# Three stages of an SSD scan, of three successive slices, issued as one row of small products

## The chip, the cores and the metric

The kernel runs on one core of a Trainium2 chip. The metric is the time of one execution on the device in microseconds (us), the median of several runs. A core has TensorE (PE) with its weight loads (PEld), VectorE (DVE), ScalarE (ACT), GpSimd (POOL) and the queues that start DMAs (SP). Each works through its own instructions in order and waits for others by semaphores.

## The reference, cut to what matters

One step of a two-layer streaming encoder. The change concerns the mixer of layer 0, a Mamba-2 SSD scan (state-space duality) over 1088 positions: 1024 of a new stream and 64 of a running one, whose state h0 is given.

```python
# ssd_mixer: u @ w_in gives z, x/B/C and dt; x/B/C go through a conv of width 4 and silu
y, h_final = ssd_scan(xs, dt, A, Bm, Cm, h0)
y = y + xs * D_skip
y = y * silu(z)
yg = y * rsqrt(mean(y * y over a group of 512 channels) + eps) * gnorm_w
return yg @ w_out

# ssd_scan, by chunks of positions; Acs is the cumulative sum of dt * A in a chunk
Lm = exp(where(causal, Acs[q] - Acs[s], -inf))
y_diag = (C B^T * Lm) @ (x * dt)                        # inside a chunk
chunk_states = B^T @ (x * dt * exp(Acs[-1] - Acs))      # what a chunk adds to the state
h[c + 1] = h[c] * exp(Acs[-1]) + chunk_states[c]        # over the chunks
y_off = (C @ h[c]) * exp(Acs)                           # from the state before
y = y_diag + y_off
```

Then follow a feed-forward layer, shared keys and values, and a layer of attention with its feed-forward layer, which the change doesn't touch.

## The kernel before, in words

**Tiles.** Positions lie along the free axis, in three slices `SL` of 384, 384 and 320, channels along the 128 partitions. The scan takes chunks of 128 positions (`CHL`, nine, the last of 64), so a slice holds three. The 2048 channels of x are 16 tiles j of two heads each. A slice of a tile is numbered q = 3 j + s, 48 in all; below, "slice q" means this.

**Large products.** `unit` (L401) makes one tile of x, z, B or C for one slice: 24 products in `passes` (L386, the rows of L394, L395 and L396), since each factor is split in a high and a low part and three of the four combinations are taken over 8 blocks of k. `passes` and `unit` go through the tiles in the loop at L1011 to L1030: x of tile j, z of tile j − 1, for each slice, and B and C for each four tiles. The result is scaled by the norm of the input (`scaled`, L677, DVE). x, B and C go through `Conv` (L687: craw, then four steps in cvt, L715 and L717, DVE, then Silu on ACT), z through Silu on ACT (tile zs). The weights are cast and split as they come in (L296 ACT, L297 DVE, tile hl).

**Small products.** `group_task` (L730) prepares B and CB of a group, `ssd_task` (L758) the scan of one slice. It is a generator of four stages:

- A: PE transposes x (xtp, L769) and spreads the cumulative sums over the partitions (bcp, L786); DVE makes xd (x dt, L779) and dm (L791), POOL xe (L780), ACT the Exp into ea (L795) and dm (L796), DVE dm times CB (L797).
- B: PE makes the states of the three chunks (sp, L805); DVE carries the state on (hn, L816, L819); for the last chunk SP loads the state of the running stream (h, L811), and hn is stored (L826, L828).
- C: PE makes the two parts of the output (yp, L836, from dm and xd; yo, L845, from the states and C); DVE makes y (L847) and ea times yo (L849), POOL adds them (L850).
- D: POOL multiplies by silu(z) (L856), SP stores y (L857), squares are summed by group in ssg (ACT L863 and L866, POOL L867). In the last tile of a group `rstd` turns these sums into the norm (nst on PE, L427, then the nv chain on DVE from L433).

**What sets the order.** PE runs in the order in which the code issues its instructions. `Stream` (L80) keeps a clock of estimated work; `passes` and `unit` advance it and let every waiting generator go on whose delay has passed and whose condition holds. This happens after each 12 large products, so stages stand between half units as rows of small products. The stages' delays, `SSD_GAP` and the counters in `so` decide between which. The instructions of the other engines are put in order by a scheduler, in which a block under `tc.high_priority(HIP)` goes first. Tiles have few buffers: xd, xe and ea two each, dm four (two per slice), y and h six, zs three, cvt one; in PSUM two each for xtp, sp and others (`ax`), for bcp, and for yp and yo.

**Behind it.** While the last slices run, `build_y` (L634) takes y up again: dg (L448) and nbp (L456) spread the norm, L541 to L543 scale and split y into r, and `project` (L656) multiplies by the output weights, in quarters of the positions, first for half of the channels. At the start, `start_norm` makes the norm of the input with the same nst, nv, dg and nbp.

Of the kernel before, what the change touches and what calls it, by code (L numbers as in the profile page):

```python
# [8 lines left out]
F32 = mybir.dt.float32  # L9
# [3 lines left out]
ALU = mybir.AluOpType  # L13
# [3 lines left out]
P = 128  # L17
D = 1024
# [11 lines left out]
CHL = [128] * 8 + [64]  # L30
HEADS = 32
XT = 16
# [8 lines left out]
RB_WAIT = 4.8  # L41
CHW = ((13.1, 8.8, 18.0), (7.5, 6.0, 17.2)), ((9.0, 5.2, 14.6), (10.5, 6.0, 19.7))
AT_W1, AT_W2 = 6.0, 2.5
SSD_GAP, SSD_D = 4.4, 6.5
ST_W, ST_RB = (6.5, 22.0, 22.0), 1.0
TB_W, TB_V = 1.0, 18.0
ES = 0.5, 0.5, 0.0
# [3 lines left out]
HIP = 3000  # L51
# [20 lines left out]
C_D = 208  # L72
# [246 lines left out]
def hybrid_kernel(  # L319
# [4 lines left out]
    nc = tc.nc  # L324
    V, A, G, PE = nc.vector, nc.scalar, nc.gpsimd, nc.tensor
    ctx.enter_context(tc.manual_schedule(engines={mybir.EngineType.PE}))
    st = Stream()
# [45 lines left out]
    def col(c):  # L373
        return pcs[:, c:c + 1]

    def ax(name):
        return pax.tile([P, 512], F32, tag="ax", name=name)
# [204 lines left out]
    with ExitStack() as es:  # L582
        pbc = es.enter_context(tc.tile_pool(reuse_waits="tile", name="pbc", bufs=2, space=PSUM))
        pyy = es.enter_context(tc.tile_pool(reuse_waits="tile", name="pyy", bufs=2, space=PSUM))
        sb1 = es.enter_context(tc.tile_pool(reuse_waits="tile", name="sb1", bufs=1))
        sb2 = es.enter_context(tc.tile_pool(reuse_waits="tile", name="sb2", bufs=2))
# [35 lines left out]
        dt, acs, dec, cd = tab("dt"), tab("acs"), tab("dec"), tab("cd")  # L622
        tabs = []
# [6 lines left out]
        def table_task():  # L630
# [31 lines left out]
            for s, (o, n) in enumerate(SL):  # L662
                ps = ax("acT")
                for i in range(3):
                    c = 3 * s + i
                    L = CHL[c]
                    PE.transpose(ps[:32, i * P:i * P + L], acs[:L, c, :], ident[:L, :L])
# [5 lines left out]
        rbs = [sb1.tile([P, 384], F32, name=f"rb{s}") for s in range(NSL)]  # L673

        def scaled(dst, ps, s, a, n):

            V.tensor_tensor(dst, ps[:, a:a + n], rbs[s][:, a:a + n], op=ALU.mult)  # L677

        def dt_unit(us, n, pl, tg):
            ps = pl.tile([P, 512], F32, tag=tg, name="dtp")  # L680
# [71 lines left out]
        bc_t = {}  # L752
        cb_done = []
        hst = {}
        so = dict(A=0, B=0, C=0, D=0, tA=0, tC=0)
        ssgs = {}

        def ssd_task(j, s):  # L758
            g, jj = divmod(j, 4)
            xsT = pair_t[j].dst[s]  # L760
            CT = grp_t[g][1].dst[s]
            o, n = SL[s]
            q = 3 * j + s
            yield 0, 0, lambda: tabs and (g, s) in cb_done and so["A"] == q and so["C"] >= q - 1 and st.t >= so["tA"]
            Bn, CB = bc_t[g, s]

            pt = ax("xtp")
            for i in range(3):
                PE.transpose(pt[:, i * P:(i + 1) * P], xsT[:, i * P:(i + 1) * P], ident)  # L769
            xd = sb2.tile([P, 3, P], F32, tag="xd", name="xd")  # L770
            xe = sb2.tile([P, 3, P], F32, tag="xe", name="xe")

            def hd(ap):
                return ap.rearrange("p a (h d) -> p a h d", d=64)

            def tb(t_):
                return t_[:, 3 * s:3 * s + 3, 2 * j:2 * j + 2].unsqueeze(3).to_broadcast([P, 3, 2, 64])

            V.tensor_tensor(hd(xd), hd(pt[:, :384].rearrange("p (a b) -> p a b", b=P)), tb(dt), op=ALU.mult)  # L779
            G.tensor_tensor(hd(xe), hd(xd), tb(dec), op=ALU.mult)  # L780
            MT = []
            ea = sb2.tile([P, 384], F32, tag="ea", name="ea")
            for e in range(2):
                hh = 2 * j + e
                bp = pbc.tile([P, 512], F32, tag="bc", name="bcp")
                PE.matmul(bp[:, :n], sel[:, hh:hh + 1].to_broadcast([P, P]), acr[:, o:o + n], start=True, stop=True)  # L786
                dm = sb2.tile([P, 384], F32, tag="dm", bufs=4, name="dm")
                for i in range(3):
                    c = 3 * s + i
                    L = CHL[c]  # L790
                    V.scalar_tensor_tensor(  # L791
                        dm[:, i * P:i * P + L], bp[:, i * P:i * P + L], acs[:, c, hh:hh + 1], mask[:, :L],
                        op0=ALU.subtract, op1=ALU.min,
                    )
                A.activation(ea[64 * e:64 * e + 64, :n], bp[64 * e:64 * e + 64, :n], AF.Exp)  # L795
                A.activation(dm[:, :n], dm[:, :n], AF.Exp)  # L796
                V.tensor_tensor(dm[:, :n], dm[:, :n], CB[:, :n], op=ALU.mult)  # L797
                MT.append(dm)
            so["A"] = q + 1
            so["tA"] = st.t + SSD_GAP  # L800
            yield 0.7, 4.5, lambda: so["B"] == q

            sp = ax("sp")
            for i in range(3):
                PE.matmul(sp[:, i * P:(i + 1) * P], Bn[:, i, :], xe[:, i, :], start=True, stop=True)  # L805
            hs = []
            for i in range(3):
                c = 3 * s + i
                if c == 8:
                    hst[j] = sb2.tile([P, P], F32, tag="h", bufs=6, name="h")  # L810
                    nc.sync.dma_start(hst[j], h0T[:, j * P:(j + 1) * P])  # L811
                h = hst.get(j)
                hs.append(h)
                hn = sb2.tile([P, P], F32, tag="h", bufs=6, name="hn")
                if c == 0:
                    V.tensor_copy(hn, sp[:, :P])  # L816
                else:
                    for e in range(2):
                        V.scalar_tensor_tensor(  # L819
                            hn[:, 64 * e:64 * e + 64], h[:, 64 * e:64 * e + 64],  # L820
                            cd[:, c, 2 * j + e:2 * j + e + 1], sp[:, i * P + 64 * e:i * P + 64 * e + 64],
                            op0=ALU.mult, op1=ALU.add,
                        )
                hst[j] = hn
                if c == 7:
                    nc.sync.dma_start(hp_o[:, j * P:(j + 1) * P], hn)  # L826
                if c == 8:
                    nc.sync.dma_start(hs_o[:, j * P:(j + 1) * P], hn)  # L828
            so["B"] = q + 1
            yield 0.8, 3.5, lambda: so["C"] == q and so["D"] >= q - 5 and st.t >= so["tC"]  # L830

            yp = pyy.tile([P, 512], F32, tag="yy", name="yp")
            for i in range(3):
                L = CHL[3 * s + i]
                for e in range(2):
                    PE.matmul(  # L836
                        yp[64 * e:64 * e + 64, i * P:i * P + L], xd[:, i, 64 * e:64 * e + 64],
                        MT[e][:, i * P:i * P + L], start=True, stop=True,
                    )
            yo = pyy.tile([P, 512], F32, tag="yy", name="yo")  # L840
            for i in range(3):
                c = 3 * s + i
                L = CHL[c]
                if c > 0:
                    PE.matmul(yo[:, i * P:i * P + L], hs[i], CT[:, i * P:i * P + L], start=True, stop=True)  # L845
            y = sb2.tile([P, 384], F32, tag="y", bufs=6, name="y")
            V.scalar_tensor_tensor(y[:, :n], xsT[:, :n], col(C_D + j), yp[:, :n], op0=ALU.mult, op1=ALU.add)  # L847
            q0 = P if s == 0 else 0
            V.tensor_tensor(ea[:, q0:n], yo[:, q0:n], ea[:, q0:n], op=ALU.mult)  # L849
            G.tensor_tensor(y[:, q0:n], y[:, q0:n], ea[:, q0:n], op=ALU.add)  # L850
            so["C"] = q + 1
            so["tC"] = st.t + SSD_GAP
            yield 1.5, 0, lambda: (j, s) in zst and so["D"] == q
            so["D"] = q + 1

            G.tensor_tensor(y[:, :n], y[:, :n], zst[j, s][:, :n], op=ALU.mult)  # L856
            nc.sync.dma_start(yd_[:, j, o:o + n], y[:, :n])  # L857
            if jj == 0 and s == 0:
                ssgs[g] = sb2.tile([P, NCH * P], F32, tag="ssg", bufs=1, name="ssg")
                G.memset(ssgs[g][:, T:], 0.0)  # L860
            ssg = ssgs[g]
            if jj == 0:
                A.activation(ssg[:, o:o + n], y[:, :n], AF.Square)  # L863
            else:
                sq = nsb.tile([P, 384], F32, tag="sq", bufs=2, name="sq")
                A.activation(sq[:, :n], y[:, :n], AF.Square)  # L866
                G.tensor_tensor(ssg[:, o:o + n], ssg[:, o:o + n], sq[:, :n], op=ALU.add)  # L867
            if jj == 3:
                yield 0, 5.0
                rstd(ssg[:, s * 384:(s + 1) * 384], 1.0 / 512, rst[:, 3 * s:3 * s + 3, g], 3)  # L870
                rst_done.add((g, s))
                yield 0.3, 0

        zst = {}
# [35 lines left out]
        for s, (o, n) in enumerate(SL):  # L910
            xs = []
            if s == 0:
                nc.sync.dma_start(pcs, pc)
                for m in range(0, KD, 3):
                    w_ = min(3, KD - m)
# [67 lines left out]
        for s in range(NSL):  # L983
            us, n = u[s], SL[s][1]
# [5 lines left out]
            for i in range(3):  # L990
                ps = mm("mm") if i else pl.tile([P, 512], F32, tag=tg, name="mmp")
# [19 lines left out]
        for grp in order:  # L1011
# [6 lines left out]
            for i, s in seq:  # L1018
                kd_, jj_ = grp[i]
                q = 3 * jj_ + s  # L1020
# [404 lines left out]
    with ExitStack() as es:  # L1425
        psS = es.enter_context(tc.tile_pool(reuse_waits="tile", name="psS", bufs=2, space=PSUM))
        sb2 = es.enter_context(tc.tile_pool(reuse_waits="tile", name="sba2", bufs=2))
# [237 lines left out]
        for j in range(1, 8):  # L1665
# [4 lines left out]
            for s in range(NSL):  # L1670
                n = SL[s][1]
# [138 lines left out]
```

## Time and profile before

| what | us |
|---|---|
| median of 3 runs | 3126.31 (3126.17 to 3128.03) |
| the profiled execution | 3128.07 |
| its span | 3126.40 |
| PE busy | 2999.5 (96%) |
| DVE busy | 2183.2 (70%) |
| ACT busy | 1361.3 (44%) |
| POOL busy | 932.8 (30%) |

The profile is of one execution. The span runs from its first instruction to its last; an engine's share is its busy time over the span. A mean over stages with different limits says little on any one of them, so the stretch of the scan, about 85 to 710 us, is read by itself. "Waits" are the times in which an engine stood idle for another, with the line that waited and the line that released it. A granted clock of 1.00 is TensorE at full speed. In the timeline, a row's first number is the start and the second the duration; products overlap, so that the distance of two starts is what a product costs.

### The profile page before, as it was taken

To read this page: it belongs to the slowest core of one execution; us is meant where nothing else is said; L and a number is where in the kernel's file an instruction comes from. 1 tells how busy PE (TensorE), PEld (TensorE's weight loads), DVE (VectorE), ACT (ScalarE), POOL (GpSimd) and SP (SyncE) were. 2 spreads that over 40 slices of the span, in tenths; PEclk is the share of its full clock that TensorE was granted. 3 is DMA by queue.
4 is the path that set the end of the run, shared out by engine and by line. 5 is a ranking of instruction groups with operands and counts; after the bars stand their busy time and mean duration, and the time that the engine had idled before them with its cause. 6 is when DMAs were issued, how large, how long until landed. Compare 5 with 4: busy or idle time off the path is not lost. (4 is left out here: it accounts for less than half of the span.)

```text
span 3126.4 us, 56643 instructions
## 1 busy us (share of the span) xinstructions
PE 2999.5 (96%) x21721; PEld 2913.4 (93%) x21721; DVE 2183.2 (70%) x4712; ACT 1361.3 (44%) x2424; POOL 932.8 (30%) x1026
## 2 busy tenths in 40 slices
PE   7999999999998999999998999999998999999998
PEld 7899999989998999999987888888998999999997
DVE  8888888886788555584566788887778655476545
ACT  5545454554443222344443554444544232244432
POOL 3333333331344433441133001100155333342112
PEclk9999999999999999999999999999999999999999
DMA  3111111124533222245654111112344222245654
GB/s 107 40 56 51 57 50 58 50 83 143 170 123 105 78 77 82 86 145 175 200 184 122 53 62 59 57 54 64 127 144 132 74 73 80 77 127 170 204 184 135
DMA packets 174495, 321.80 MB, mean 103 GB/s; under 512 B 17136, under 2 KB 124528, under 8 KB 174224
## 3 DMA queue, kind: packets, MB, share of 16 engines
q1 hardware_dynamic: 174160, 318.11, 32.7%
q8 instruction: 171, 2.80, 0.4%
q14 instruction: 100, 0.82, 0.1%
q0 software_dynamic: 64, 0.07, 0.0%
HBM read 255.51 MB, written 62.60 MB: 102 GB/s over the span
## 5 line engine op out<-in xcount | busy, mean ns | idle before, releaser
L297 DVE TENSOR_TENSOR hl<-raw,hl 128x1024 fp32r<-128x1024 f32 (+1 forms) x297 | 366.0, 1233 | 323.4 <-ACT hl L296 319.8
L394 PE MATMUL mm<-r,hl 128*128 128x384 f32 (+2 forms) x1664 | 563.2, 338 | 10.1 <-DVE kf L1469 9.1
L396 PE MATMUL mm<-r,hl 128*128 128x384 f32 (+2 forms) x1664 | 541.9, 326 | 1.1 <-DVE hl L297 1.1
L395 PE MATMUL mm<-r,hl 128*128 128x384 f32 (+2 forms) x1664 | 541.3, 325 | 0.0
L296 ACT CAST hl<-raw 128x1024 fp32r<-128x1024 f32 (+1 forms) x300 | 303.5, 1014 | 316.8 <-DMA raw<-in_w_f_dram 125.8
L420 POOL TENSOR_TENSOR ssum<-ssum,sq 128x288 f32<-128x288 f32 (+3 forms) x188 | 221.9, 1183 | 565.4 <-ACT sq L419 559.4
L1209 PE MATMUL px<-r,hl 128*128 128x288 f32 (+1 forms) x1192 | 349.6, 293 | 0.0
L394 PEld LDWEIGHTS mm<-r,hl 128*128 128x128 f32 x1664 | 318.1, 191 | 18.8 <-issue 8.2
L395 PEld LDWEIGHTS mm<-r,hl 128*128 128x128 f32 x1664 | 318.3, 191 | 0.9 <-issue 0.5
L396 PEld LDWEIGHTS mm<-r,hl 128*128 128x128 f32 x1664 | 317.3, 191 | 1.4 <-DVE hl L297 1.4
L1208 PE MATMUL px<-r,hl 128*128 128x288 f32 x1056 | 311.4, 295 | 4.4 <-DVE u L1223 4.4
L1210 PE MATMUL px<-r,hl 128*128 128x288 f32 x1056 | 310.7, 294 | 0.0
L1210 PE MATMUL px<-rx,hl 128*128 128x256 f32 x816 | 230.4, 282 | 17.9 <-DVE hl L297 17.9
L1208 PE MATMUL px<-rx,hl 128*128 128x256 f32 x816 | 230.8, 283 | 0.7 <-ACT hl L296 0.7
L1209 PEld LDWEIGHTS px<-r,hl 128*128 128x128 f32 x1192 | 223.9, 188 | 0.0
L1370 PE MATMUL po<-rx,hl 128*128 128x384 f32 (+1 forms) x640 | 207.1, 324 | 0.9 <-DVE rx L1272 0.9
L1208 PEld LDWEIGHTS px<-r,hl 128*128 128x128 f32 x1056 | 198.4, 188 | 6.0 <-DVE u L1223 5.8
L1371 PE MATMUL po<-rx,hl 128*128 128x384 f32 (+1 forms) x608 | 197.0, 324 | 2.0 <-DVE hl L297 2.0
L1369 PE MATMUL po<-rx,hl 128*128 128x384 f32 (+1 forms) x608 | 198.6, 327 | 0.1
L1210 PEld LDWEIGHTS px<-r,hl 128*128 128x128 f32 x1056 | 198.3, 188 | 0.0
L1209 PE MATMUL px<-rx,hl 128*128 128x256 f32 x680 | 191.8, 282 | 0.0
L256 POOL TENSOR_TENSOR tt<-raw 128x512 f32<-128x512 f32 x44 | 61.5, 1397 | 426.3 <-DMA raw<-in_w_f_dram 287.0
(337 smaller groups left out, 8136.0 us busy)
## 6 DMA issues: line engine op xcount, KB each, us to landing
raw<-in_w_f_dram SPq DMA_DIRECT2D x204, 512.0 KB, 3.7
raw<-in_w_in_dram SPq DMA_DIRECT2D x40, 512.0 KB, 3.7
raw<-in_w_f_dram SPq DMA_DIRECT2D x48, 384.0 KB, 3.2
sg<-hscr SPq DMA_DIRECT2D x88, 192.0 KB, 3.5
raw<-in_w_so_dram SPq DMA_DIRECT2D x32, 512.0 KB, 3.8
raw<-in_w_kv_dram SPq DMA_DIRECT2D x16, 512.0 KB, 3.7
raw<-in_w_o_dram SPq DMA_DIRECT2D x16, 512.0 KB, 3.8
sg<-hscr SPq DMA_DIRECT2D x44, 160.0 KB, 3.6
```

What stands on the lines that cost most here:

```text
L296: self.nc.scalar.copy(h, v)
L297: (eng or self.eng or self.nc.vector).tensor_tensor(lo, v, h, op=ALU.subtract)
L394: PE.matmul(ps[:, :n], h_, xh, start=(first and i == 0), stop=False)
L395: PE.matmul(ps[:, :n], h_, xl, start=False, stop=False)
L396: PE.matmul(ps[:, :n], l_, xh, start=False, stop=(last and i == nk - 1))
L420: (eng or G).tensor_tensor(ssum[:, :n], ssum[:, :n], q[:, :n], op=ALU.add)
L1208: PE.matmul(ps, wh, ah[:, k, :], start=(k == 0), stop=False)
L1209: PE.matmul(ps, wh, al[:, k, :], start=False, stop=False)
L1210: PE.matmul(ps, wl, ah[:, k, :], start=False, stop=(k == 3))
L1369: PE.matmul(ps[:, :n], wh, xh, start=(k == 0), stop=False)
L1370: PE.matmul(ps[:, :n], wh, xl, start=False, stop=False)
L1371: PE.matmul(ps[:, :n], wl, xh, start=False, stop=(k == FT - 1))
```

## The change

B and C of a slice become functions, `states` and `outputs`, kept in `stages[q]`. When A of slice q is issued, C of slice q − 2 and B of slice q − 1 are issued just ahead of it, so that a row holds C, B and A of three successive slices. The distance of two rows grows with `SSD_GAP` from 4.4 to 9.5; `SSD_W` and `SSD_E` are the delays after which a slice's later stages are issued by themselves, should no further A have done it. A may run up to two slices ahead of C (before, one), and D must wait for its C. The evacuation `scaled` gets the high priority.

```diff
-SSD_GAP, SSD_D = 4.4, 6.5
+SSD_GAP, SSD_D = 9.5, 6.5
+
+SSD_W, SSD_E = (15.0, 14.0), (4.5, 3.5)
...
         def scaled(dst, ps, s, a, n):
-            V.tensor_tensor(dst, ps[:, a:a + n], rbs[s][:, a:a + n], op=ALU.mult)
+            with tc.high_priority(HIP):
+                V.tensor_tensor(dst, ps[:, a:a + n], rbs[s][:, a:a + n], op=ALU.mult)
...
+        stages = {}
+
+        def later(q, key):
+            if so[key] != q or q not in stages or (key == "C" and so["B"] <= q):
+                return 0
+            cost = stages[q][key]()
+            so[key] = q + 1
+            return cost
...
-            yield 0, 0, lambda: tabs and (g, s) in cb_done and so["A"] == q and so["C"] >= q - 1 and st.t >= so["tA"]
+            yield 0, 0, lambda: (
+                tabs and (g, s) in cb_done and so["A"] == q and so["C"] >= q - 2 and st.t >= so["tA"]
+                and so["D"] >= q - 7
+            )
+
+            cost = 0.7 + later(q - 2, "C") + later(q - 1, "B")
...
             so["tA"] = st.t + SSD_GAP
-            yield 0.7, 4.5, lambda: so["B"] == q
+            def states():       # B: sp, hn, the DMAs of the states, as before
...
-            yield 0.8, 3.5, lambda: so["C"] == q and so["D"] >= q - 5 and st.t >= so["tC"]
+            def outputs():      # C: yp, yo, y, ea, as before
...
-            yield 1.5, 0, lambda: (j, s) in zst and so["D"] == q
+            out = {}
+            stages[q] = dict(B=states, C=outputs)
+
+            w_ = SSD_E if q == 3 * XT - 1 else SSD_W
+            yield cost, w_[0]
+            yield later(q - 1, "C") + later(q, "B"), w_[1] if so["C"] == q else 0, lambda: so["D"] >= q - 5
+            yield later(q, "C"), 0, lambda: (j, s) in zst and so["D"] == q and so["C"] > q
```

What it makes of the order, at three places. On PE in the steady part, four successive rows of small products before (the large products between them are left out):

```order
L805 MATMUL sp<-xe,Bn 128x128 x3
...
L769 MATMUL xtp<-ident,xsT 128x128 x3
L786 MATMUL bcp<-acr,sel 128x384 x2
...
L836 MATMUL yp<-dm,xd 64x128 x4
L836 MATMUL yp<-dm,xd 64x64 x2
L845 MATMUL yo<-CT,hn 128x128 x2
L845 MATMUL yo<-CT,h 128x64
...
L805 MATMUL sp<-xe,Bn 128x128 x3
```

and a row in the same part now:

```order
L856 MATMUL yp<-dm,xd 64x128 x4
L856 MATMUL yp<-dm,xd 64x64 x2
L865 MATMUL yo<-CT,hn 128x128 x2
L865 MATMUL yo<-CT,h 128x64
L823 MATMUL sp<-xe,Bn 128x128 x3
L787 MATMUL xtp<-ident,xsT 128x128 x3
L804 MATMUL bcp<-acr,sel 128x384 x2
```

B, A and C stood 12 large products apart here; in other places before, two or three of them stood together. Now every row has all three, 48 large products behind the row before it. Before, five rows held three slices' stages, now three do.

On PE in the tail, between units of the first projection, the rows around the norm of the last tile before (nst; six, for two slices):

```order
L394 MATMUL mm<-r,hl 128x256
L395 MATMUL mm<-r,hl 128x256
L396 MATMUL mm<-r,hl 128x256
L427 MATMUL nst<-ones,ssg 128x1 x6
L456 MATMUL nbp<-dg,frac 128x256
L394 MATMUL mm<-r,hl 128x256
```

and now:

```order
L398 MATMUL mm<-r,hl 128x256
L856 MATMUL yp<-dm,xd 64x128 x4
L856 MATMUL yp<-dm,xd 64x64 x2
L865 MATMUL yo<-CT,hn 128x128 x2
L865 MATMUL yo<-CT,h 128x64
L458 MATMUL nbp<-dg,frac 128x256
L396 MATMUL mm<-r,hl 128x256
```

The last slice's C now stands ahead of that nbp. Three nst follow 12 large products behind it, and the six stand 96 large products behind their old place; before, the three stood 24 products behind the six. In large products, the last slice's A moved 36 later and the last three C's 48 to 60.

On DVE at the start, the norms of the second and third slices (nv, nr, dg; x2 is twice in a row) behind the conv steps (cvt) before:

```order
L717 SCALAR_TENSOR_TENSOR cvt<-craw,pcs,cvt 128x384 x3
L433 TENSOR_SCALAR nv<-nst 128x3 x2
L434 TENSOR_SCALAR nv<-nv 128x3 x2
L437 TENSOR_TENSOR nv<-nv 128x3 x2
...
L444 SCALAR_TENSOR_TENSOR nr<-nv 128x3 x2
L448 TENSOR_TENSOR dg<-ident,nr 128x384 x2
```

and now:

```order
L720 SCALAR_TENSOR_TENSOR cvt<-craw,pcs,cvt 128x384
L435 TENSOR_SCALAR nv<-nst 128x3 x2
L436 TENSOR_SCALAR nv<-nv 128x3
L720 SCALAR_TENSOR_TENSOR cvt<-craw,pcs,cvt 128x384
L439 TENSOR_TENSOR nv<-nv 128x3
L436 TENSOR_SCALAR nv<-nv 128x3
L720 SCALAR_TENSOR_TENSOR cvt<-craw,pcs,cvt 128x384
```

Two conv steps moved from ahead of the chain into it. In the same part PE's first rows, before A of slice 0, A of slice 1, B, C of slice 0, are now A of slice 0, B of slice 0, A of slice 1, C of slice 0.

More of the change, by code (lines that the diff above doesn't have):

```diff
@@ L754, in hybrid_kernel @@
         hst = {}
-        so = dict(A=0, B=0, C=0, D=0, tA=0, tC=0)
+        so = dict(A=0, B=0, C=0, D=0, tA=0)
         ssgs = {}
+        stages = {}
[5 more added lines that the diff above has]
+            return cost
         def ssd_task(j, s):
@@ L800, in ssd_task @@
             so["tA"] = st.t + SSD_GAP
-            yield 0.7, 4.5, lambda: so["B"] == q
[L803 to L817, printed above, removed]
+            def states():
+                sp = ax("sp")
+                for i in range(3):
+                    PE.matmul(sp[:, i * P:(i + 1) * P], Bn[:, i, :], xe[:, i, :], start=True, stop=True)
+                hs = []
+                for i in range(3):
+                    c = 3 * s + i
+                    if c == 8:
+                        hst[j] = sb2.tile([P, P], F32, tag="h", bufs=6, name="h")
+                        nc.sync.dma_start(hst[j], h0T[:, j * P:(j + 1) * P])
+                    h = hst.get(j)
+                    hs.append(h)
+                    hn = sb2.tile([P, P], F32, tag="h", bufs=6, name="hn")
+                    if c == 0:
+                        V.tensor_copy(hn, sp[:, :P])
+                    else:
+                        for e in range(2):
+                            V.scalar_tensor_tensor(
+                                hn[:, 64 * e:64 * e + 64], h[:, 64 * e:64 * e + 64],
+                                cd[:, c, 2 * j + e:2 * j + e + 1], sp[:, i * P + 64 * e:i * P + 64 * e + 64],
+                                op0=ALU.mult, op1=ALU.add,
+                            )
+                    hst[j] = hn
+                    if c == 7:
+                        nc.sync.dma_start(hp_o[:, j * P:(j + 1) * P], hn)
+                    if c == 8:
+                        nc.sync.dma_start(hs_o[:, j * P:(j + 1) * P], hn)
+                out["hs"] = hs
+                return 0.8
@@ L818, in ssd_task @@
+            def outputs():
+                hs = out["hs"]
+                yp = pyy.tile([P, 512], F32, tag="yy", name="yp")
+                for i in range(3):
+                    L = CHL[3 * s + i]
                     for e in range(2):
[L819 to L822, printed above, removed]
-                        )
@@ L824, in ssd_task @@
[L824 to L829, printed above, removed]
-            yield 0.8, 3.5, lambda: so["C"] == q and so["D"] >= q - 5 and st.t >= so["tC"]
[L832 to L852, printed above, removed]
-            yield 1.5, 0, lambda: (j, s) in zst and so["D"] == q
+                        PE.matmul(
+                            yp[64 * e:64 * e + 64, i * P:i * P + L], xd[:, i, 64 * e:64 * e + 64],
+                            MT[e][:, i * P:i * P + L], start=True, stop=True,
+                        )
@@ new lines, in outputs @@
+                yo = pyy.tile([P, 512], F32, tag="yy", name="yo")
+                for i in range(3):
+                    c = 3 * s + i
+                    L = CHL[c]
+                    if c > 0:
+                        PE.matmul(yo[:, i * P:i * P + L], hs[i], CT[:, i * P:i * P + L], start=True, stop=True)
+                y = out["y"] = sb2.tile([P, 384], F32, tag="y", bufs=6, name="y")
+                V.scalar_tensor_tensor(y[:, :n], xsT[:, :n], col(C_D + j), yp[:, :n], op0=ALU.mult, op1=ALU.add)
@@ new lines, in outputs @@
+                q0 = P if s == 0 else 0
+                V.tensor_tensor(ea[:, q0:n], yo[:, q0:n], ea[:, q0:n], op=ALU.mult)
+                G.tensor_tensor(y[:, q0:n], y[:, q0:n], ea[:, q0:n], op=ALU.add)
+                return 1.5
+            out = {}
[3 more added lines that the diff above has]
+            yield later(q - 1, "C") + later(q, "B"), w_[1] if so["C"] == q else 0, lambda: so["D"] >= q - 5
@@ L854, in ssd_task @@
+            yield later(q, "C"), 0, lambda: (j, s) in zst and so["D"] == q and so["C"] > q
+            y = out["y"]
             so["D"] = q + 1
```

## The prediction

> **What bounds the kernel now.** I read the page first, then the waits of PE, then stretches of the span by engine, and last PE's instructions one by one where small products stand between large ones.
>
> ```profile
> span 3126.4 us, 56643 instructions
> PE 2999.5 (96%) x21721; PEld 2913.4 (93%) x21721; DVE 2183.2 (70%) x4712; ACT 1361.3 (44%) x2424; POOL 932.8 (30%) x1026
> ```
>
> PE is busy for 96% of the span, so only PE's own time or PE's waits can move the end. The order of work differs between about 85 and 710 us alone (layer 0); everything behind that stands in the same order on every engine. Three stretches matter: the first slices (to 110 us), the steady part (110 to 660 us) and the tail (660 to 710 us), in which the last slices meet the first units of the output projection. The waits of PE (total us, times, longest us), first up to 110 us, then in the tail:
>
> ```profile
> PE nbp L456 <- DVE dg L448: 7.0, 2, 6.2
> PE bcp L786 <- ACT ea L795: 1.0, 2, 0.7
> ```
>
> ```profile
> PE nst L427 <- POOL ssg L867: 1.7, 2, 1.4
> PE nbp L456 <- DVE nv L433: 1.5, 1, 1.5
> PE yo L845 <- DMA h<-in_h0T_dram: 1.1, 1, 1.1
> PE mm L394 <- ACT r L563: 1.0, 1, 1.0
> PE bcp L786 <- ACT ea L795: 0.8, 2, 0.5
> ```
>
> Between 110 and 660 us the same view lists no wait of PE at all. Busy time by stretch says how near the others are (PE, PEld, DVE, ACT, POOL, then the granted clock, the DMA share, GB/s):
>
> ```profile
> 300.00:400.00 100.00, 100.00 (x692) 97.39 (x691) 82.60 (x207) 51.96 (x82) 34.32 (x68) 1.00 0.16 51
> 685.00:690.00 5.00, 5.00 (x37) 4.81 (x35) 4.88 (x8) 3.03 (x7) 2.66 (x3) 1.00 0.40 113
> 690.00:695.00 5.00, 1.87 (x14) 1.68 (x14) 5.00 (x9) 2.73 (x5) 3.27 (x4) 0.92 0.44 133
> 695.00:700.00 5.00, 5.00 (x22) 4.82 (x23) 4.44 (x23) 0.88 (x2) 1.38 (x2) 0.50 0.72 206
> ```
>
> In the steady part PE never rests at full clock, and DVE has 17.4 us in 100 to spare. In the tail DVE is full (4.88 and 5.00 of 5.00) while PE falls to 1.87 of 5.00, and then the clock is 0.50 for 5 us. That clock costs about 2.5 us there and 0.4 us in the stretch before (8% of 5), 2.9 us together; the waits add up to 6.1 us.
>
> **Steady part: joining rows.** The change takes nothing from PE: both orders hold the same products. Before, three successive slices have five rows of small products between large ones, 80 rows over 48 slices; now three, 48 rows. So 32 interruptions of the large products go. Whether one has a price of its own is read from rows of one kind and of several. First C and B of two slices, then B and A, then B alone, then C, B and A together (start, duration):
>
> ```profile
> 304.55 0.34 PE L396 MATMUL mm<-r,hl 128*128 128x384 f32 x1
> 304.82 0.77 PE L836 MATMUL yp<-dm,xd 128*64 128x128 f32 x12
> ...
> 306.88 0.42 PE L394 MATMUL mm<-r,hl 128*128 128x384 f32 x1
> 307.14 0.34 PE L395 MATMUL mm<-r,hl 128*128 128x384 f32 x1
> ```
>
> ```profile
> 298.70 0.33 PE L394 MATMUL mm<-r,hl 128*128 128x384 f32 x1
> 298.87 0.33 PE L395 MATMUL mm<-r,hl 128*128 128x384 f32 x1
> 299.05 0.34 PE L396 MATMUL mm<-r,hl 128*128 128x384 f32 x1
> 299.22 0.83 PE L805 MATMUL sp<-xe,Bn 128*128 128x128 f32 x6
> 299.89 0.49 PE L769 MATMUL xtp<-ident,xsT 128*128 128x128 f32 x3
> 300.13 0.59 PE L786 MATMUL bcp<-acr,sel 128*128 128x384 f32 x2
> 300.56 0.33 PE L394 MATMUL mm<-r,hl 128*128 128x384 f32 x1
> 300.74 0.34 PE L395 MATMUL mm<-r,hl 128*128 128x384 f32 x1
> ```
>
> ```profile
> 318.08 0.31 PE L396 MATMUL mm<-r,hl 128*128 128x320 f32 x1
> 318.23 0.83 PE L805 MATMUL sp<-xe,Bn 128*128 128x128 f32 x6
> 318.81 0.42 PE L394 MATMUL mm<-r,hl 128*128 128x384 f32 x1
> 319.07 0.34 PE L395 MATMUL mm<-r,hl 128*128 128x384 f32 x1
> ```
>
> ```profile
> 115.90 0.34 PE L396 MATMUL mm<-r,hl 128*128 128x384 f32 x1
> 116.17 0.77 PE L836 MATMUL yp<-dm,xd 128*64 128x128 f32 x12
> ...
> 119.00 0.30 PE L394 MATMUL mm<-r,hl 128*128 128x320 f32 x1
> 119.14 0.31 PE L395 MATMUL mm<-r,hl 128*128 128x320 f32 x1
> 119.28 0.30 PE L396 MATMUL mm<-r,hl 128*128 128x320 f32 x1
> ```
>
> Neighbouring large products start 0.175 us apart at 384 columns (298.70 to 299.05 is two steps) and 0.14 us at 320 (119.00 to 119.28). The cost of a row is the time from the start of the large product ahead of it to the start of the second one behind it, less these two steps: CB 307.14 − 304.55 − 0.35 = 2.24 us, BA 300.74 − 299.05 − 0.35 = 1.34, B 319.07 − 318.08 − 0.14 − 0.175 = 0.675, CBA 119.14 − 115.90 − 0.175 − 0.14 = 2.925. If a row had a price of its own, CBA would be cheaper than its parts. A is 1.34 − 0.675 = 0.665, and CB + A = 2.905, against 2.925 measured. The cost is additive to 0.02 us. So the saving per row that goes is 0 to 0.02 us, at most 0.6 us over 32 rows. I take −0.4 us. The reason is seen in the starts: the hole is at the entry to yp (304.55 to 304.82 is 0.27, not 0.175, +0.095) and at the exit after sp (306.88 to 307.14 is 0.26, +0.085), while B enters in 0.15 and A is left in 0.18. Each of the 48 C's keeps its entry to yp.
>
> The rule of "Perfetto Trace Analysis" (section Identifying the Most-Contended Engine) in the Trainium skill, that TensorE's room is judged by the share of time in which weights are loaded, speaks for more room than I grant (the far end of the second rival). The rows say that this room stands at yp, whichever row it is in.
>
> **Steady part: the deeper pipeline.** A, B and C of a slice now stand one row apart each. A row stands at every 48 large products: a third of the rows has a 320-column slice, so 48 × 0.163 + 2.9 = 10.7 us, and A to C is two of them. xd, xe and ea have two buffers (dm four, two for a slice), so A of slice q writes into what C of q−2, at the head of the same row, is still reading. New waits follow: on ACT the Exp into ea (L795) waits for POOL's addition (L850), which waits for DVE's L847 and L849.
>
> ```profile
> L717 DVE SCALAR_TENSOR_TENSOR cvt<-craw,pcs,cvt 128x384 f32<-128x384 f32 (+1 forms) x186 | 113.7, 611 | 1.8
> L847 DVE SCALAR_TENSOR_TENSOR y<-xsT,pcs,yp 128x384 f32<-128x384 f32 (+1 forms) x45 | 26.4, 587 | 17.1 <-PE yp L836 16.6
> L850 POOL TENSOR_TENSOR y<-y,ea 128x384 f32<-128x384 f32 (+2 forms) x44 | 44.9, 1020 | 66.1 <-DVE ea L849 50.4 <-DVE nv L444 11.6 <-ACT dm L796 3.3
> ```
>
> That chain is 0.59 for y, no more than that for ea (fewer operands, same width) and 1.02 on POOL, 2.2 us after yp. Behind the Exp on ACT are queued dm's Exp, the Silu of x and z and the casts of the weights; behind xd's product on DVE are the splits of the same weights. PE asks for none of it before the next row, 10.7 us on, and the convs of DVE's queue (four steps of 0.61) fit in between. DVE has 0.174 × 10.7 = 1.9 us a row to spare. So I price this at 0; without that cover each microsecond over 1.9 goes straight to PE (third rival). The high priority of the evacuation L677 frees PSUM sooner, which PE never waits for between 110 and 660 us: 0.
>
> **Start.** B of slice 0 now stands ahead of A of slice 1, which puts a product that waits for xe in front of one whose own wait (bcp on ea, 1.0 in two) would then partly be spent: down to −1.0. Against it, the reordered DVE queue puts two steps of cvt (0.61 each) inside the chain nv to dg, on which nbp waits (6.2 and 0.8): up to +1.2. The second end is the more certain, as PE already waits at that place: +0.5 us.
>
> **Tail.** A of the last slices stands 48 products apart, so bcp's 0.8 goes. The six nst that wait 1.7 for POOL and hold nbp 1.5 stand 96 large products later, and three others, for an earlier slice, stand 24 products behind their old place; PE no longer stops there first. What is late next is r: DVE, full from 685 to 695 us, has the same splits, conv steps and normalisations to do, and the last three C's, moved 48 to 60 large products later, add y and ea to exactly this stretch. The products that follow need r (1.0 now) and h, whose load (1.1) starts only when SP has passed the store of the state before it. So I let most of the 5.3 us come back as waits for these, and of the clock's 2.9 us I take 1.6 off: −0.8 − 1.6 = −2.4 us. The ends are −9.0 (all 6.1 and 2.9 gone) and +4.5 (nothing gained, and r late by as long as the nst and nbp chain is now: 1.7 + 1.5, with 1.3 of more half clock).
>
> On that clock "TensorE: Matmul & The Clock Gate" (Part 1) in the Trainium skill says that it drops to half after an idle window of about 3.4 us whose phase runs free. The trace agrees: 0.50 in 695 to 700 after 3.1 us of idling in the five before.
>
> **Sum.** −0.4 + 0 + 0.5 − 2.4 = −2.3 us. The profiled execution took 3128.07 us, its span being 3126.4; it becomes 3125.8. It lies 1.8 above the median of the runs, 3126.31, so in the median I forecast 3124.0 us.
>
> **Rivals.**
> First, the tail clears: with nst and nbp off their place, PE runs through, all waits and the half clock go. −0.4 + 0.5 − 9.0 = −8.9: 3117.4 us. For it: 3.2 of 6.1 us hang on rows that move. Against: DVE is full there. 0.15.
>
> Second, an interruption does have a price that additivity of a few rows hides (entry 0.095 and exit 0.085, 0.18 for each of 32): −5.8 + 0.5 − 2.4 = −7.7, 3118.6 us. For it: the holes exist. Against: 2.905 and 2.925 above. At its furthest, all the time in which PEld rests (2.61 in 100 us) would be won over 550 us: −14.4, 3111.9 us. 0.08, of which 0.02 for that end.
>
> Third, slower: the two-buffer tiles hold the queues. C, B and A now release y, ea, hn, xd and dm in one burst, in which xd of q waits on DVE behind y and ea of q−2, ACT's Exp waits for POOL, and the casts of weights and the evacuations behind them come late. It decides when a row loses over 1.9 us on DVE: at 0.3 us more than that, on 44 rows, +13.2, 3137.2 us. For it: DVE at 83% is the next engine, and the weights' splits share its queue. Against: 10.7 us of cover. 0.12.
>
> The Trainium skill's "TensorE: Matmul & The Clock Gate" (its opening table) has ScalarE, VectorE and GpSimdE take their queues strictly in order, which speaks for this rival. No wait listed here shows it in the steady part.
>
> That the change doesn't do what it says is excluded by the order of PE's rows.
>
> **The numbers.** The forecast has 0.65. A measurement of this kernel can tell about 0.2%, 6.3 us: 3120.1 to 3132.6 is the same. The first two rivals are faster, 0.23; the third is slower, 0.12. The forecast's ends are 3126.3 − 0.6 − 1.0 − 9.0 = 3115.7 and 3126.3 + 1.2 + 4.5 = 3132.0. Range 3116 to 3132, with the third rival left out.
>
> **What would show it.** In the changed profile: CBA rows at 2.9 us each; no wait of PE from 110 to 660 us; DVE's share there within 1 us of 82.6; nbp's wait at the start 0.5 to 1 us longer; in the tail the nst wait gone, one on r or h larger, and less than 5 us at half clock. Wrong, if PE lists waits for xd, dm, bcp or weights (hl) in the steady part, if a row costs clearly under 2.8 us, or if PE runs through the tail.

## The result, and the profile after

The changed kernel takes 3152.9 us in the median of 4 runs (3144.72 to 3156.55), beside 3127.17 us before (4 runs, 3126.17 to 3130.91): a ratio of 1.0076, 95% interval 1.0055 to 1.0098. By this ratio it is slower by about 24 us, where I had forecast 2 us less, and it lies outside the range of 3116 to 3132 us. The profiled execution took 3156.55 us, 28.5 more than that of before. The page:

```profile
span 3154.6 us, 56701 instructions
PE 3011.6 (95%) x21721; PEld 2924.7 (93%) x21721; DVE 2194.8 (70%) x4712; ACT 1362.3 (43%) x2424; POOL 935.3 (30%) x1026
```

PE's busy time grew by 12 us for the same instructions; so a part of the loss is time at half clock, the rest is waits. The waits of PE from 110 to 660 us, where before had none, and then those of the tail (to 730 us):

```profile
PE nst L429 <- DVE hn L837: 5.0, 3, 3.9
PE nst L429 <- POOL ssg L894: 4.0, 2, 2.0
PE cbp L750 <- DVE Bn L745: 2.3, 2, 1.2
PE cbp L750 <- ACT hl L298: 1.4, 1, 1.4
```

```profile
PE nbp L458 <- DVE hn L837: 3.7, 1, 3.7
PE yo L865 <- DMA h<-in_h0T_dram: 1.6, 1, 1.6
PE mm L396 <- ACT r L544: 0.4, 1, 0.4
```

The steady part has 12.7 us of waits, and no row names yp, sp, xtp or bcp, the rows that the change joined. The names are those of the small steps that come once for a group of four tiles: its norm (nst) and its B and C (cbp). Stretches of 100 us (PE, PEld, DVE, ACT, POOL, clock, DMA share, GB/s):

```profile
200.00:300.00 100.00, 94.92 (x646) 91.92 (x643) 79.36 (x210) 45.30 (x71) 26.98 (x58) 0.97 0.14 45
300.00:400.00 100.00, 98.91 (x681) 96.03 (x680) 89.51 (x206) 51.60 (x81) 34.62 (x65) 1.00 0.17 53
400.00:500.00 100.00, 97.45 (x677) 93.97 (x676) 79.00 (x222) 54.96 (x84) 34.42 (x59) 0.98 0.16 53
500.00:600.00 100.00, 96.05 (x651) 93.03 (x650) 79.14 (x215) 46.22 (x74) 32.45 (x62) 0.98 0.15 48
```

The clock was 1.00 in these stretches before. Now 3 + 2 + 2 = 7 us are lost to it, each time behind one of the longer waits (3.9, 2.0 and 2.0 us).

Both kernels issue the same large products in the same order, so the start of the n-th one can be compared. Before, n = 624 started at 188.7 us, 1104 at 293.0, 1824 at 451.4, 2640 at 631.5 and 3264 (scan and first projection over) at 745.6. How much later (us) they start in the other kernels (e1 to e12 are the experiments below; the ratio is to runs of the kernel before that were made along with each):

| kernel | 624 | 1104 | 1824 | 2640 | 3264 | ratio to before, 95% interval |
|---|---|---|---|---|---|---|
| changed | −4.0 | 7.0 | 10.2 | 16.3 | 20.9 | 1.0076 (1.0055 to 1.0098) |
| e1 | −4.4 | 0.1 | −1.4 | 0.2 | 4.3 | 1.0023 (1.0013 to 1.0034) |
| e2 | −6.4 | 2.7 | 7.6 | 11.1 | 18.7 | 1.0076 (1.0061 to 1.0091) |
| e3 | −3.9 | 2.7 | 4.7 | 10.0 | 14.1 | 1.0070 (1.0055 to 1.0085) |
| e4 | 2.4 | 2.3 | 2.3 | 2.3 | 0.3 | 1.0005 (0.9994 to 1.0016) |
| e5 | −5.5 | −2.4 | −5.2 | −5.2 | 1.6 | 1.0020 (1.0011 to 1.0029) |
| e6 | −4.2 | 9.0 | 24.0 | 37.3 | 44.3 | 1.0151 (1.0135 to 1.0167) |
| e7 | −3.5 | −0.4 | −3.2 | −3.2 | 6.7 | 1.0029 (1.0017 to 1.0042) |
| e8 | −5.8 | −2.7 | −5.5 | −5.5 | 6.8 | 1.0041 (1.0029 to 1.0053) |
| e9 | −5.6 | 5.4 | 8.5 | 12.9 | 16.2 | 1.0094 (1.0070 to 1.0118) |
| e10 | −0.5 | 5.6 | 6.2 | 11.2 | 15.0 | 1.0064 (1.0045 to 1.0083) |
| e11 | −3.9 | −0.8 | −3.6 | −3.6 | 1.0 | 1.0014 (1.0004 to 1.0025) |
| e12 | −1.2 | 1.9 | 3.5 | 9.4 | 14.4 | 1.0038 (1.0023 to 1.0053) |

The −4.0 at 624 is no gain. By that product the changed kernel has issued two C's, one B and one A less (96 yp rows in place of 120, 54 sp in place of 60), by the prices of the prediction 2 × 1.565 + 0.675 + 0.665 = 4.5 us, owed until the tail. It owes the same at 1824 and at 2640 and nothing at 3264. At 1104 it owes only one C, so that this column can't be set against its neighbours. So the start cost +0.4 us, the steady part 16.3 + 4.0 = 20.3, which is 12.7 of waits and 7 of clock, and the tail 20.9 − 16.3 − 4.5 = 0.1. Behind the scan every engine has the same order in both programs; there the profiled execution lost 7 us more, with 85.5 us at half clock beside 66.7. No change of order explains that part: e4, in which PE has the order of before from end to end, shows 77.0 us there.

**The rows themselves** cost what I had worked out. A row with C, B and A in the steady part:

```profile
318.90 0.31 PE L398 MATMUL mm<-r,hl 128*128 128x320 f32 x1
319.14 0.77 PE L856 MATMUL yp<-dm,xd 128*64 128x128 f32 x12
...
321.97 0.30 PE L396 MATMUL mm<-r,hl 128*128 128x320 f32 x1
322.11 0.31 PE L397 MATMUL mm<-r,hl 128*128 128x320 f32 x1
```

322.11 − 318.90 − 2 × 0.14 = 2.93 us; 2.925 was the forecast.

**The largest wait** stands where a joined row is followed at once by nst. PE:

```profile
257.31 0.88 PE L856 MATMUL yp<-dm,xd 128*64 128x128 f32 x12
258.12 0.71 PE L865 MATMUL yo<-CT,hn 128*128 128x128 f32 x4
258.67 0.83 PE L823 MATMUL sp<-xe,Bn 128*128 128x128 f32 x6
259.34 0.49 PE L787 MATMUL xtp<-ident,xsT 128*128 128x128 f32 x3
259.58 0.54 PE L804 MATMUL bcp<-acr,sel 128*128 128x320 f32 x2
263.98 0.77 PE L429 MATMUL nst<-ones,ssg 128*128 128x1 f32 x3 [3.85 <-DVE hn L837]
```

and DVE in that time:

```profile
259.50 0.60 DVE L867 SCALAR_TENSOR_TENSOR y<-xsT,pcs,yp 128x384 f32<-128x384 f32 x1
260.02 0.47 DVE L718 TENSOR_SCALAR cvt<-craw,pcs 128x384 f32<-128x384 f32 x1
260.41 0.41 DVE L869 TENSOR_TENSOR ea<-yo,ea 128x256 f32<-128x256 f32 x1
260.74 0.60 DVE L720 SCALAR_TENSOR_TENSOR cvt<-craw,pcs,cvt 128x384 f32<-128x384 f32 x1
261.27 0.27 DVE L837 SCALAR_TENSOR_TENSOR hn<-hn,cd,sp 128x64 f32<-128x64 f32 x1
...
262.99 0.84 DVE L837 SCALAR_TENSOR_TENSOR hn<-hn,cd,sp 128x64 f32<-128x64 f32 x4
```

nst doesn't read hn. But sp, xtp, nst, bnp, cbp and nbp share a ring of two PSUM tiles. The row has just filled both with sp and xtp, so nst needs sp's tile, and that is held until DVE's sixth step of hn at 263.8 us, behind y, ea and the conv steps. Before, at least 24 large products lay between sp and nst. At a group's end the changed rows are not whole and not 48 apart: at 219 us yp, yo and sp stand together with bnp, cbp follows 12 large products behind, and A comes by itself at 235 us. cbp reads neither Bn nor hl: it waits for DVE's copy out of bnp's tile (Bn). The row that names hl is such a wait too, as the copy ends at 553.64 us and hl on ACT at 553.65, beside each other.

DVE's queue is also longer than it was. Between large products 624 and 2640 the same 153 conv steps (cvt) took 691 ns in the mean, before 608, which is 12.7 us. Of those above 800 ns there are 30, before 8, and all of them run for 0.4 us or more beside an addition or product of POOL. But 14 of the shorter ones before did so too, and no run shows that POOL makes them longer.

### The profile page after: what moved, and what is told of

It reads as the page before. It is cut to its first block, busy times and chain, and to the rows that moved or that the text cites. A ratio compares the mean times of both kernels' runs of the same rounds, so it can differ in the third digit from the quotient of the medians.

```text
span 3154.6 us, 56701 instructions
## 1 busy us (share of the span) xinstructions
PE 3011.6 (95%) x21721; PEld 2924.7 (93%) x21721; DVE 2194.8 (70%) x4712; ACT 1362.3 (43%) x2424; POOL 935.3 (30%) x1026
```

## The experiments

Theory 1: a small step close behind a joined row waits for the PSUM tile that sp or bnp still holds. Theory 2: the high priority of the evacuation makes hn late on DVE. Theory 3: with the deeper pipeline the sums in ssg come too late for nst. All runs but e4 start from the changed kernel.

**e1, another ring for nst.**

```diff
-                rstd(ssg[...], 1.0 / 512, rst[...], 3)
+                rstd(ssg[...], 1.0 / 512, rst[...], 3, sp=pyy.tile([P, 512], F32, tag="yy", name="nst"))
```

> The changed kernel, in which the nst of the scan takes its PSUM tile from the ring of yp and yo and no longer from that of sp, xtp, bnp, cbp and nbp. Theory 1 (a small step that stands close behind a joined row waits for the tile that sp still holds, until DVE has made hn): the waits of nst for hn between 110 and 660 us (5.0 us) fall under 0.5, the half clock behind the largest (6.8 us long, 3.4 us lost) goes, the other waits stay (nst for ssg 4.0, cbp 3.7, nbp in the tail 3.7); about 8 us less than the changed kernel, 3145 us. Theory 2 (DVE's queue is late because the evacuation goes first): nst waits over 2 us for y or ea in its place, and the time stays within 3 us of the changed kernel.

3133.49 us beside 3128.05 (the kernel before, in the same series): some 17 us of the 24 are gone, twice what I expected. By the traces half of that, 5.0 us of waits for hn and 3.4 of half clock, is what theory 1 forecast. The waits of PE from 110 to 660 us are now only cbp's, unchanged:

```profile
PE cbp L750 <- DVE Bn L745: 2.3, 2, 1.2
PE cbp L750 <- ACT hl L298: 1.4, 1, 1.4
```

The hn waits went, as theory 1 has it. The ssg waits went too, 4.0 us and 3.4 of half clock, which it does not say: those nst stand 60 large products behind a row, and ssg is what they read. ACT's order shows how. Two lines of the changed kernel, on either side of the two Exp of ea and dm, and then PE's nst:

```profile
420.00 1.28 ACT L813 ACT_TABLE_LOAD   x1 [1.75 <-DVE nv L444]
...
424.57 0.47 ACT L909 ACTIVATE zs<-zs 128x320 f32<-128x320 f32 x1
```

```profile
428.93 0.83 PE L429 MATMUL nst<-ones,ssg 128*128 128x1 f32 x6 [2.00 <-POOL ssg L894]
```

The Silu of z stands behind the Exps, which wait for DVE. In e1 the scheduler put the same Silu ahead of them, and POOL's addition into ssg, at 418.03, is over just as nst starts:

```profile
413.85 0.46 ACT L910 ACTIVATE zs<-zs 128x320 f32<-128x320 f32 x1
414.33 1.28 ACT L813 ACT_TABLE_LOAD   x1
```

```profile
418.96 0.83 PE L429 MATMUL nst<-ones,ssg 128*128 128x1 f32 x6
```

The Trainium skill says in "TensorE: Matmul & The Clock Gate" (its opening table) that ScalarE takes its queue strictly in order. The trace agrees: DVE had the Silu's operand ready at 421.2 us, and it began at 424.57, behind the Exps.

**e2, no priority; e4, before with the priority alone.**

```diff
-            with tc.high_priority(HIP):
-                V.tensor_tensor(dst, ps[:, a:a + n], rbs[s][:, a:a + n], op=ALU.mult)
+            V.tensor_tensor(dst, ps[:, a:a + n], rbs[s][:, a:a + n], op=ALU.mult)
```

> The changed kernel without the high priority of the evacuation. Theory 1: the waits of nst for hn stay at 4 to 6 us between 110 and 660 us and the time within 4 us of the changed kernel. Theory 2: these waits, and cbp's for Bn, fall under 2 us together, and the time falls by 8 us or more.

> The kernel before with the high priority of the evacuation alone. Theory 1: within 4 us of before. Theory 2: slower than before by over 6 us, with waits of PE for hn or Bn between 110 and 660 us, where before has none.

e2: 3150.51 us, 1.0076, as the changed kernel. nst waits 4.1 us for hn and 4.6 for ssg, nbp 5.5. e4: 1.0005, no difference, and no wait of PE from 110 to 660 us. Theory 2 falls.

**e3, nst later.**

```diff
-                yield 0, 5.0
+                yield 0, 9.0
```

> The changed kernel with the nst issued 9.0 instead of 5.0 units of the emission clock behind stage D. The nst of the first group that stood directly behind a joined row stands 12 large products behind it, and the last nst of the second and third groups, which stood ahead of a joined row and waited 2.0 us each for ssg, stand directly behind one. Theory 1: the 3.9 us wait of the first group falls under 1, and the two others wait 3 to 4 us each for hn instead of 2.0 for ssg; the time is about the same as the changed kernel's. Theory 3 (the sums in ssg come later by the deeper pipeline and that alone is what is late): the waits for ssg go, no new ones come, about 8 us less.

3149.04 us. The waits for ssg are gone, and these stand in their place:

```profile
PE nst L429 <- DVE hn L837: 5.9, 3, 2.2
```

In the first group nst, 12 large products behind the row, still waits 2.2 us (I expected under 1). In the other two groups, now directly behind a row, it waits 1.85 us each (expected 3 to 4). The kind is that of theory 1, the sizes are not: sp's tile is held as long as DVE's queue makes it. For theory 3 stands that later nst find ssg ready. By the profiled execution the steady part loses 13.9 us instead of 20.3; the medians, 3149.04 and 3152.9 us, don't tell the two kernels apart.

**e5, three steps in the other ring.** nst, cbp and, for the tail, nbp.

```diff
-            ps = ax("cbp")
+            ps = pyy.tile([P, 512], F32, tag="yy", name="cbp")
...
-        bp = ax("nbp")
+        bp = ax("nbp") if yyb[0] is None else yyb[0]("nbp")
```

> The changed kernel in which nst of the scan, cbp, and nbp of the tail take their PSUM tiles from the ring of yp and yo. Theory 1 (what costs is the shared ring of two tiles behind a joined row): beside e1, cbp's waits (3.7 us) go, nbp's wait of 3.7 falls to 1 or less, since y is read by DVE ahead of hn, and the half clock behind it goes (3.4): 7 to 10 us less than e1, about 3124 us, 2 to 6 us less than before. Rival (the ring only shows what another queue makes late): as much comes back as waits of PE for y, ea, r or h at the same places, and the time stays within 3 us of e1, 3133 us.

3131.3 us beside 3125.35. The steady part has no wait left, and between large products 624 and 2640 the kernel loses 0.3 us to before: with the ring out of the way joining rows costs nothing and gains nothing. What is left is in the tail and behind the scan. In the tail the rival was right, as nbp now waits for a tile that y is read from:

```profile
PE nbp L460 <- DVE y L869: 6.3, 3, 2.6
PE mm L396 <- ACT r L546: 0.8, 1, 0.8
```

**e6, the deeper pipeline without joined rows.** C, B and A of a set 12 products apart.

```diff
-            cost = 0.7 + later(q - 2, "C") + later(q - 1, "B")
+            yield later(q - 2, "C"), 0.1
+            yield later(q - 1, "B"), 0.1
+            cost = 0.7
...
-SSD_GAP, SSD_D = 9.5, 6.5
+SSD_GAP, SSD_D = 5.0, 6.5
```

> The changed kernel's deeper pipeline without its joined rows: C, B and A are issued in the same sequence, 12 large products apart (SSD_GAP 5.0 to keep a set each 48 to 60), with the old ring. Some 2 in 3 of the joints are opened, 90 rows more. Theory 1: nst, which then finds at most one of the two tiles taken a short time before, waits for hn 1 us or less in all between 110 and 660 us (5.0 in the changed kernel); where xtp is put behind sp and bnp, it waits instead, 2 to 4 us at a place. If a row has a price of 0 to 0.02 us, the steady part loses 0 to 2 us to the opened joints; with the price of 0.18 us (second rival of the prediction) 16 us. If the deeper pipeline were the cost and not the joint, the waits of nst would stay as they are. About 3138 us by theory 1 with no price of a row.

3174.23 us, much slower than expected:

```profile
PE nst L429 <- POOL ssg L896: 17.3, 3, 5.8
PE xtp L789 <- DVE hn L839: 9.1, 3, 3.1
```

Three things are told apart. nst no longer waits for hn; but xtp, issued behind sp and bnp, does, in three places for 3 us each, as the ring predicts. Between the group ends, from product 1104 to 1344, five sets with two joints opened in each take 0.1 us less than in e5 (as many stages, of slices one apart): a row has no price of its own, and the second rival of the prediction falls. And the sums come later still, so that the waits for ssg are 5.8 us each: these don't need the joint. Much of the loss is clock, 37.5 us at half in the steady part.

**e7, nbp back in the old ring but away from rows; e8, the same with a short end.**

```diff
-                yield 0, 4.0
+                yield 0, 4.0, lambda: st.t >= tr[0] + 6.0
...
-            w_ = SSD_E if q == 3 * XT - 1 else SSD_W
+            w_ = SSD_E if q >= 3 * XT - 3 else SSD_W
```

(The second piece is in e8 alone; tr[0] is the time of the last row.)

> The changed kernel with nst and cbp in the ring of yp and yo, and with nbp of the tail back in the old ring but issued no sooner than 6 units of the emission clock behind a row of small products (some 24 large products behind its start and more). Theory 1 (place and ring make the tail's wait): no wait of PE between 110 and 660 us, the tail's waits for y or hn (6.3 us in the run with three in the other ring) fall to 1 or less in all, r stays under 1.5, and the half clock of the tail shortens from 10.2 to 3.4 us; about 8 us less than that run, 2 to 3 us below before. Rival (DVE is full in the tail, and what is taken from one wait comes back as another): waits for r, h or nst grow to 4 us or more, and the time stays within 3 us of that run, 4 to 8 us above before.

> The same, and the last three slices issue their B and C by themselves after 4.5 and 3.5 units of the emission clock, so that the pipeline is short again at the end of the scan, as before. If what the tail loses is that the last C's stand 48 to 60 large products later than before, their y, ea and squares fall ahead of the splits of r, and the tail's waits come to no more than before's 6.1 us, with the time 2 to 5 us under the run without this. If DVE's load sets the tail whatever the order, no difference beyond 2 us.

e7: 3136.24 us beside 3126.05; e8: 3138.14. In e7 the wait for nbp is gone and is back as r:

```profile
PE mm L396 <- ACT r L545: 6.6, 4, 2.3
PE mm L397 <- DVE r L546: 0.8, 3, 0.3
PE nbp L458 <- DVE hn L840: 0.2, 1, 0.2
```

In e8, r waits 3.1 and nst 4.1 us. Both gain nothing, as the rival had it: with a later nbp it is r that is late, and at product 3264 the two stand 6.7 and 6.8 us behind before, e5 1.6.

**e9, z's Silu first.**

```diff
-                    A.activation(zst[i, s][:, :n], zst[i, s][:, :n], AF.Silu)
+                    with tc.high_priority(HIP):
+                        A.activation(zst[i, s][:, :n], zst[i, s][:, :n], AF.Silu)
```

> The changed kernel with the Silu of z at high priority on ACT. The theory for the two waits of nst for ssg (2.0 us each): on ACT the two Exp of ea, which wait for DVE, stand ahead of z's Silu, so that y times z on POOL, the square and ssg come late. By it both waits go, with the half clock behind each (1.7 us lost each); the waits for hn (5.0) and of cbp stay; some 7 us less than the changed kernel, 3146 us. Against it stand 24 more table loads of ACT, 1.28 us each, on an engine half of whose time is free: no cost by the theory. If the sums are late for another reason (POOL, or the squares), the waits stay at 3 us or more.

3152.58 us, four executions from 3143.86 to 3163.0: no gain that could be told. The ssg waits halve, to 1.0 us each. ACT's rows show why no more than half goes:

```profile
422.76 1.28 ACT L910 ACT_TABLE_LOAD   x1
424.06 0.47 ACT L910 ACTIVATE zs<-zs 128x320 f32<-128x320 f32 x1
424.55 1.28 ACT L814 ACT_TABLE_LOAD   x1
...
427.34 0.46 ACT L893 ACTIVATE sq<-y 128x320 f32<-128x320 f32 x1
```

Silu and Exp have a table load of 1.28 us between them each time, and the Silu still comes behind the first Exp. The square it was to hasten then stands behind the second Exp, which the two loads have made later. My "no cost" was wrong. cbp's waits grow from 3.7 to 5.9 us; no table load stands near them, and why they grow is not shown. That the ssg waits hang on ACT's order is shown in part by e1 and this run.

**e10, hn first on DVE.**

```diff
-                        for e in range(2):
-                            V.scalar_tensor_tensor(
+                        with tc.high_priority(HIP):
+                            for e in range(2):
+                                V.scalar_tensor_tensor(
```

> The changed kernel with the steps of hn on DVE at high priority, so that no conv step stands between them; the rings and PE's order are as in the changed kernel. Theory 1 with DVE's queue as the size of the wait (nst stands 0.7 us behind sp and waits until the last of six hn steps has read it; of the 4.4 us from sp to the last hn, about 2.2 us are conv steps between them): the longest wait of nst for hn falls from 3.9 to 1 to 2 us, nbp's in the tail from 3.7 to 1 to 2, and the waits of cbp, which follow Bn, do not grow; the time falls by 5 to 10 us, to about 3145 us. If the tile's order in the ring and not the time of DVE were the cause, the waits stay over 3 us.

3147.68 us. With rings and PE's order unchanged, the six steps of hn stand together, and the three hn waits of 5.0 us become one of 1.7:

```profile
262.46 1.22 DVE L838 SCALAR_TENSOR_TENSOR hn<-hn,cd,sp 128x64 f32<-128x64 f32 x6
```

```profile
PE nst L429 <- POOL ssg L895: 5.4, 2, 2.7
PE nst L429 <- DVE hn L838: 1.7, 1, 1.7
PE cbp L750 <- DVE Bn L745: 0.7, 2, 0.4
```

So the wait is the ring's, and DVE's queue sets its length. The waits for ssg grow by 1.4 us, which I had not expected.

**e11, three steps in the other ring, and a short end; e12, what the runs pointed to.** e11 is e5 with the short end of e8; e12 has nst and cbp in the other ring, nbp in the old one, hn first, and the short end.

> The kernel with nst, cbp and nbp in the ring of yp and yo, and with B and C of the last three slices issued by themselves after 4.5 and 3.5 units. Between 110 and 660 us no wait of PE. If the place of the last C's makes the loss of the tail, its waits fall from 7.1 us to under 4 and the kernel stands at or under before. If what DVE has to do there sets the end, they come back under another name, as in the run with nbp apart, and the time stays 4 to 8 us above before.

> What the runs point to, together: nst and cbp in the ring of yp and yo, nbp in the old one (in the run before, yo waited 4.5 us for the tile that nbp held), hn at high priority, B and C of the last three slices issued soon. No wait of PE between 110 and 660 us. If the wait of yo for nbp's tile was all that stood in the tail, its waits come to 2 us or less (nbp for hn at most 1.4) and the time to 3 to 5 us under that run, at or just under before. If DVE's load sets the tail, 3 us or more come back as r, nst or nv, and the time stays 3 to 6 us above before.

e11: 3129.03 us beside 3125.29, the nearest to before but not at it. Its tail still waits 5.6 us in all, under other names, as I had written for the case that DVE's load sets the end. Most of it is yo, which waits for the tile of nbp, since nbp is now in yo's ring:

```profile
PE yo L867 <- ACT rb L464: 4.5, 1, 4.5
```

e12: 3143.04 us beside 3130.51, by the ratios some 8 us over e11, where I had expected less than e11. Without that wait others came in the tail (r 2.4, nst 2.0, nbp 1.4). In the steady part one row is left, though nst and cbp are out of the old ring:

```profile
PE nst L429 <- POOL ssg L895: 5.4, 2, 2.7
```

e10 has the same two waits, so they came with hn's priority, and z's Silu stands behind the Exps again. The waits for ssg are thus a second cause beside the ring. No version beat the kernel before.

## Why the prediction was wrong, point by point

- **"The change takes nothing from PE", rows at −0.4 us.** Right: 2.93 us for a row against 2.925, and +0.3 us over the steady part in e5. The second rival fell with it.
- **Start, +0.5 us.** +0.4 us. The smaller wait of nbp grew from 0.8 to 1.6 us, sp now waits for xe, and bcp's 1.0 went, as these rows of the changed kernel up to 110 us show:

```profile
PE nbp L458 <- DVE nr L446: 1.6, 1, 1.6
PE sp L823 <- POOL xe L798: 1.0, 1, 1.0
```

- **"So I price this at 0" (the deeper pipeline).** This is the step that failed: the steady part lost 20.3 us. It rested on "PE asks for none of it before the next row", which doesn't hold at a group's end, where nst and cbp ask sooner. Some 12 of the 20 us are the ring's: 5.0 of waits for hn, 3.7 of cbp's and 3.4 of half clock. The step looked at xd, xe, ea and dm, the buffers that A, B and C hand to each other; none of them made PE wait from 110 to 660 us, but for 0.7 us of bcp for ea in e9. It didn't look at the PSUM ring of two tiles, which sp and xtp share with the steps of a group, and it took the order of PE only from stretches without a group's end. There nst or cbp stood 0 to 12 large products behind small products that had just taken both tiles. e1, e5 and e10 show the ring as the cause (move the step to another ring, or make the tile's reader sooner), e2 and e4 clear the priority, e6 shows that the depth alone doesn't make nst wait for hn. Some 7 of the 20 us are the waits for ssg, 4.0 and 3.4 of half clock. There nst asks for sums that wait for the Silu of z, which I had named as queued behind the Exps. e12 shows such waits without the ring; why ACT's queue has the Silu ahead of the Exps in some kernels and behind them in others stays open.
- **The third rival (queues held)** forecast the right sign, 3137 us, on a condition that wasn't met: a row's 1.9 us to spare on DVE were not used up. The longer conv steps took 12.7 us over the steady part, some 0.3 us a row. DVE's busy share fell from 82.5 to 79.4 between 200 and 300 us, where PE waited, and rose from 82.6 to 89.5 between 300 and 400, where I had forecast no change beyond 1 us. A piece of the rival did appear, in the ssg waits: ACT's Exp waits for DVE with z's Silu behind it.
- **"No wait of PE from 110 to 660 us"** was the sign that I named for being wrong, with xd, dm, bcp or weights as suspects. None of the four was it; the one row that names hl is cbp's, which reads no weights and whose wait went with the ring in e5. The half clock behind the waits I had priced in the tail alone: 7 us in the steady part.
- **Tail, −2.4 us.** +0.1 us in the changed kernel, by the prices of the rows. I had forecast less than 5 us at half clock; it was 10.2, before 6.8. That DVE and r are what is late next was right: in e7 the 6.3 us of waits came back as 7.4 us for r. r itself waited only 0.4 us in the changed kernel. What was not seen is that nbp would stand right behind the last full row and wait 3.7 us for sp's tile, the mechanism of the steady part once more.

## What to carry to other kernels

Before joining small steps on an engine, list every ring of buffers that they draw on and everything else that draws on it, and look for the rare steps too, those of a group's end. A ring of two that is filled by one row makes the next user wait until one of the two tiles has been read, though it needs none of that data. Then ask of each rare step which results it reads itself, and what now stands ahead of them in the other queues. The average row, priced rightly, tells nothing of either: the steady rows cost 0, and a few places cost 20 us.

## What the runs showed of the hardware

- The order of small products between large ones costs PE only the sum of its parts: a joined row takes 2.93 us, and five of them opened at two joints each took 0.1 us less in all.
- Waits of 2.0 to 3.9 us on PE were each followed, in the changed kernel, by 3.4 or 6.8 us at a granted clock of half, so that a wait cost up to nearly twice its length. The length alone doesn't decide it. In e10 a wait of 1.7 us at 264 us was followed by such a stretch. Two waits of nst for ssg took 2.7 us each there, at 426 and at 588 us, and only the second was followed by a lower clock (the column behind the busy times).

```profile
420.00:432.00 12.00, 9.30 (x68) 8.80 (x67) 9.72 (x29) 4.76 (x9) 3.86 (x8) 1.00 0.31 102
584.00:596.00 12.00, 9.30 (x59) 8.63 (x58) 7.91 (x28) 2.62 (x4) 4.70 (x8) 0.86 0.26 94
```

  The Trainium skill says in "TensorE: Matmul & The Clock Gate" (Part 1) that the window which is watched runs free, so that the same kernel meets it at different phases. The two rows are in line with that; they don't show the window itself.
